# Strassen's seven products for the first layer's branch columns of the input projection

## The chip, the core and the metric

The kernel runs on one core of a Trainium2 chip. A core has five engines that run side by side, each with its own queue of instructions: TensorE (PE in the profile) multiplies matrices into PSUM; VectorE (DVE), ScalarE (ACT) and GpSimd (POOL) do elementwise work; SyncE (SP) issues most of the DMA transfers here. Engines wait for each other through semaphores, and an engine that waits holds up all that stands behind in its queue. The metric is the device time of one execution in microseconds, as the median of several runs.

## The reference

The model is a backbone of two layers over 512 latent tokens and 256 context tokens, all in float32 with 1024 channels. One layer computes:

```
h       = RMSNorm(stream) * (1 + scale) + shift          # shift, scale, gate from SiLU(c) @ w_ada
B C X Z | q k v ZA | GLA q k v r ZG | merge gates = h @ w_in
conv    = B * conv3(C * X) * silu(Z)                     # -> w_br_conv
attn    = attention(q, k, v) * silu(ZA)                  # -> w_br_attn, 8 query heads, 2 key heads
gla     = RMSNorm(gated_linear_attention) * silu(ZG)     # -> w_br_gla, 4 heads, both directions
stream += gate * RMSNorm((sum of sigmoid(merge gate) * branch) @ w_out)
```

In layer 0 latent and context tokens both go on (768 tokens), in layer 1 the output needs the 512 latent ones alone.

## The kernel before, in words

**Products.** A float32 product is carried by three products of shorter parts: each operand is split into a high part, which the multiplier holds exactly, and the rest (`sub_parts`: a cast on ACT, a subtraction on DVE), and `PARTS` lists which parts meet. A column of the input projection (`col_steps`, `gemm_a`, L208) is 128 output channels for all tokens: eight blocks of 128 input channels, three products each, and in layer 0 each product in two pieces of 512 and 256 tokens, so 48 matmuls into one tile `psA` of a ring of three. Its 128 columns of weights are 512 KB, a `Unit`: one DMA into a ring of three `raw` buffers, then a split into a ring of four `hl` buffers.

**Two streams.** The program is a list of `Step`s. The main stream holds the conv columns C, X, Z, B of each of eight channel blocks (`conv_y`), the branch projections (`branch`, with the merge gates' columns), the gated attention (`gated_y`: a ZA column, its SiLU times u, a split) and the last branch (`branch_c`). The side streams hold attention, the four GLA heads (`gla`, with ZG, and levels of decayed blocks: `build` on DVE, one group of products, one masked copy), and the modulation of the next layer (`ada_rows`, L288). `weave` puts side steps between main ones in proportion to the slack that a table gives each. After that every engine has a fixed order. `advance` issues loads and splits of the weights ahead of their steps, as far as the rings allow by a running sum of step costs. Stores go into a list `later` and are issued one step behind.

**Buffers.** Rings in SBUF: H (16 tiles of 128x768), G (16), M (2), `raw` (3), `hl` (4). A tile of a ring can be written again only when all that read its predecessor is done. Attention's and GLA's results `u_att`, `u_gla` and the running sum of the branches `mg` are kept in DRAM and read back.

**The start.** The program loads and normalises the four latent token blocks; the shift and scale of two channel blocks come at a time (`ada_quarter`, L340, four quarters). For each pair of channel blocks the normalised tokens are transposed on PE, scaled and split (`make_h`, `make_h_low`), and the first four columns run piece by piece behind these quarters. The context blocks are normalised meanwhile.

**The end of layer 0.** The last branch's `gating` steps multiply SiLU(ZG) by u_gla, split the product, and the branch's columns `rest` follow. `w_out` then gives the new stream.

## Time and profile before

| | |
|---|---|
| median of 3 runs | 2436.82 us (2435.99 to 2437.19) |
| span of the profiled execution | 2433.6 us |
| PE busy | 2379.5 us, 98%, 14039 matmuls |
| DVE, ACT, POOL busy | 1213.7 (50%), 912.2 (37%), 301.7 us (12%) |
| DMA | 224.26 MB, mean 92 GB/s |
| granted PE clock, mean | 0.995 |

The span runs from the first to the last instruction of one profiled execution; the runs' times also hold what lies around it. Busy shares are means over stages with different limits. In the views that follow, a row of the groups reads: line, engine, operation, output and inputs by the program's names, shapes, count, then busy time and mean duration in ns of one instruction, then the idle time of that engine before them and what ended it. A row of the windows gives for each engine the busy microseconds and the count in one stretch, then the PE clock that was granted, the share of the DMA engines and GB/s. Rows of the chain and of the timeline begin with a start time and a duration. A row on DMA ends with the median time from issue to landing. Layer 0 takes the first 1430 us or so.

### The profile page before, as it was taken

Reading aid. Unit: us, or ns where it says so; the run is one execution under the profiler, and the core shown is the slowest. Engines: PE = TensorE matmul, PEld = TensorE weight load, DVE = VectorE, ACT = ScalarE, POOL = GpSimd, SP = SyncE. Lnnn points to the kernel's source line nnn. Section 1 sums busy time; section 2 is a strip of 40 time slices with the busy share of each in tenths; the row PEclk is TensorE's granted clock in tenths of the full one; section 3 lists DMA queues with packets and bytes.
Section 4 is the critical chain, followed back from the end, with each engine's and each line's share of the span. In section 5 each row is a group of like instructions: output and inputs, shape, how many; then the busy total and the mean of one; then the engine's idle time right before and its main releaser. Section 6 shows DMA issues by size and latency. Waiting matters only on the chain.

```text
span 2433.6 us, 34123 instructions
## 1 busy us (share of the span) xinstructions
PE 2379.5 (98%) x14039; PEld 2059.3 (85%) x14039; DVE 1213.7 (50%) x1910; ACT 912.2 (37%) x1415; POOL 301.7 (12%) x354
## 2 busy tenths in 40 slices
PE   6999999999999999999999989999999999999998
PEld 4899989899988898888988878888888888878877
...
GB/s 244 97 54 52 65 53 77 53 75 76 57 76 119 112 96 128 79 107 84 83 78 99 123 93 97 61 80 88 69 65 87 98 98 122 96 147 62 117 112 109
DMA packets 311080, 224.26 MB, mean 92 GB/s; under 512 B 16600, under 2 KB 281612, under 8 KB 310924
## 3 DMA queue, kind: packets, MB, share of 16 engines
...
q8 instruction: 110, 1.80, 0.3%
...
## 4 chain that ended last, share of the span: by engine, by line
PE 52%; DVE 3%; issue 1%; ACT 1%; DMA 1%; POOL 1%; SPq 0%; POOLq 0%; DVEq 0%; ACTq 0%
PE psA L208 32%; PE psA L216 6%; PE psA L1079 2%; PE psA L716 2%; PE psB L216 2%; PE psB L583 1%; PE psA L824 1%; PE psA L144 1%; PE psA L547 1%; DMA u<-u_gla 1%; DVE hl L125 1%; PE psA L801 1%; PE psB L288 1%; PE psB L1107 1%; ACT junk L158 0%
## 5 line engine op out<-in xcount | busy, mean ns | idle before, releaser
L208 PE MATMUL psA<-hT,hl 128*128 128x512 f32 x5952 | 1211.6, 358 | 3.1 <-DVE hl L125 1.0
L208 PEld LDWEIGHTS psA<-hT,hl 128*128 128x128 f32 x5952 | 967.4, 189 | 177.6 <-issue 15.5
L125 DVE TENSOR_TENSOR hl<-raw,hl 128x1024 fp32r<-128x1024 f32 x258 | 323.2, 1264 | 333.1 <-ACT hl L129 329.9
L129 ACT CAST hl<-raw 128x1024 fp32r<-128x1024 f32 x258 | 266.5, 1047 | 108.8 <-DMA raw<-in_w_in 58.1
L208 PE MATMUL psA<-hi,hl 128*128 128x512 f32 (+1 forms) x1152 | 305.0, 361 | 0.0
L216 PE MATMUL psA<-hl,hT 128*128 128x256 f32 x1920 | 233.7, 283 | 0.0
L216 PEld LDWEIGHTS psA<-hl,hT 128*128 128x128 f32 x1920 | 232.2, 192 | 1.8 <-issue 0.7
L208 PEld LDWEIGHTS psA<-hi,hl 128*128 128x128 f32 x1152 | 190.2, 188 | 35.2 <-issue 1.7
L208 PE MATMUL psA<-lo,hl 128*128 128x512 f32 x576 | 175.1, 358 | 1.1 <-DVE lo L125 1.1
L125 POOL TENSOR_TENSOR rstd<-ms,mhalf 128x1 f32<-128x1 f32 (+4 forms) x54 | 48.8, 904 | 781.2 <-DVE ms L153 632.8
L125 POOL TENSOR_TENSOR Sf<-Sf,a 128x384 f32<-128x384 f32 x56 | 60.8, 1085 | 670.5 <-DVE K L125 425.1
L552 ACT ACTIVATE pe<-psA,nmx 128x768 f32<-128x768 f32 (+1 forms) x80 | 65.4, 817 | 128.1 <-DVE nmx L550 126.0
L208 PEld LDWEIGHTS psA<-lo,hl 128*128 128x128 f32 x576 | 95.0, 188 | 18.1 <-DVE lo L125 1.8
L549 DVE TENSOR_REDUCE mx<-psA 128x1 f32<-128x768 f32 (+1 forms) x80 | 67.8, 847 | 63.5 <-PE psA L547 63.5
L125 DVE TENSOR_TENSOR pTlo<-psA,pThi 128x768 fp32r<-128x768 f32 (+1 forms) x72 | 63.8, 924 | 70.1 <-ACT pThi L129 69.3
L216 PE MATMUL psB<-hl,hT 128*128 128x256 f32 x768 | 94.6, 283 | 0.0
L216 PEld LDWEIGHTS psB<-hl,hT 128*128 128x128 f32 x768 | 93.5, 191 | 1.0
L125 DVE TENSOR_TENSOR sg<-sg,psA 128x768 f32<-128x768 f32 (+1 forms) x48 | 39.3, 819 | 78.9 <-PE psA L208 75.0
L129 ACT CAST pThi<-psA 128x768 fp32r<-128x768 f32 (+1 forms) x72 | 52.8, 779 | 67.7 <-PE psA L144 67.7
L913 POOL TENSOR_SCALAR cv<-u,vec 128x768 f32<-128x768 f32 (+1 forms) x16 | 37.1, 2321 | 307.9 <-DVE u L125 307.9
L464 DVE TENSOR_REDUCE ss<-sq 128x4 f32<-128x512 f32 (+1 forms) x32 | 18.8, 586 | 111.5 <-ACT sq L463 111.5
L125 POOL TENSOR_TENSOR Pb<-Pb,a 128x384 f32<-128x384 f32 x56 | 66.9, 1194 | 0.0
...
## 6 DMA issues: line engine op xcount, KB each, us to landing
raw<-in_w_in SPq DMA_DIRECT2D x192, 512.0 KB, 3.8
raw<-in_w_ada SPq DMA_DIRECT2D x64, 256.0 KB, 2.7
raw<-in_w_br_conv SPq DMA_DIRECT2D x16, 512.0 KB, 4.1
raw<-in_w_br_attn SPq DMA_DIRECT2D x16, 512.0 KB, 4.4
raw<-in_w_br_gla SPq DMA_DIRECT2D x16, 512.0 KB, 4.4
raw<-in_w_out SPq DMA_DIRECT2D x16, 512.0 KB, 4.3
wada<-in_w_ada SPq DMA_DIRECT2D x16, 384.0 KB, 6.5
mg<-sg SPq DMA_DIRECT2D x16, 384.0 KB, 3.7
```

Source lines behind the costliest of these rows:

```text
L125: e.tensor_tensor(out=o, in0=a, in1=b, op=op)
L129: act.copy(out=hi, in_=src)
L144: nc.tensor.transpose(o, i, ident[:n, :n])
L208: mm(ps[:, c0:c0 + wd], lhsT=w[a][:, kb, :], rhs=pair[s], start=(kb == 0 and i == 0), stop=(kb == NK - 1 and i == 2))
L216: mm(ps, lhsT=h_block(kb, tb, a), rhs=w[s][:, kb % 4, :], start=(kb == 0 and i == 0), stop=(kb == NK - 1 and i == 2))
L288: mm(ps[rj:rj + 32, :], lhsT=cst[:, n * i + g, :], rhs=us[n * i + g].raw[j], start=True, stop=True, tile_position=(0, rj))
L547: mm(ps[:, c0:c1], lhsT=Q[j][a][:, qs], rhs=K["k"][b][:, c0:c1], start=(i == 0), stop=(i == 2))
L549: dve.tensor_reduce(out=mx, in_=ps[:, k0:NT], axis=AX.X, op=ALU.max)
L552: act.activation(out=pe[:, k0:], in_=ps[:, k0:NT], func=AF.Exp, bias=nmx, scale=SCALE, accum_out=sm)
L716: mm(ps[:, cs], lhsT=K[:, cs], rhs=Q[:, cs], start=True, stop=True)
L913: pl.tensor_scalar(out=c["cv"][:, :nq], in0=u[:, :nq], scalar1=tap(1), scalar2=None, op0=ALU.mult)
L1079: mm(ps0[tb], lhsT=merged[kb][a][:, ts_], rhs=u0[i].val[b][:, k, :], start=(kb == 0 and z == 0), stop=(kb == NK - 1 and z == 2))
```

## The change

Only layer 0 changes its products. Its columns of the branches (conv C, X, Z, B of channel blocks 1 to 7, the 24 merge gates, ZA and ZG: 68 columns) are made in 34 pairs (`pair_steps`). A pair is two weight blocks of 128 columns, a and b. Input channels are taken in couples of blocks, tokens in two halves of 384. For three of the four couples (`NQ = 3`) the product of a 2x2 arrangement (two columns by two channel blocks, with two token halves) is made by Strassen's scheme in Winograd's form, with seven products instead of eight: p1 to p7, of which p1, p6, p7 and p4 add up in one PSUM bank half U. The fourth couple is multiplied as before (`plain`). All matmuls of a pair are 384 wide, and there are 87 of them where the two columns had 96.

The scheme needs sums of weight blocks, made on POOL in the `raw` buffers (`prep_s`), and sums of token halves of h, made once at the start (`first_h`, tiles TX, 12 of the 16 H tiles). The two operands of the conv product are combined as before. The pairs for Z of the paths and for the merge gates apply their function and store the result in DRAM (`sp0` to `sp5`): y of the conv branch, three gates, two SiLU gates. `load_y` reads y back before branch 0, and u_att and SiLU(ZA) before branch 1; `branch` and `branch_c` read the gates. Now all the pairs come first in the main stream, then the branches.

Besides: h of a channel block is one tile for all 768 tokens; at the start all six token blocks are normalised and transposed before the first modulation quarter; the G ring has 14 tiles, and four of its tiles instead of eight may hold weights ahead of their use; rotary tables are loaded for each pair of query heads; GLA's value columns come after levels 4 and 5; attention and all four heads of layer 0 are woven as one side stream.

```diff
-AHEAD = {"raw": RAW_BUFS, "G": 8, "hl": HL_BUFS, "wo": 4}
+AHEAD = {"raw": RAW_BUFS, "G": 4, "hl": HL_BUFS, "wo": 4, "none": 99}
...
-        return pool.tile([P, NT], dt, tag="G", bufs=16, name=name)
+        return pool.tile([P, NT], dt, tag="G", bufs=14, name=name)
...
+        raws, val = [], {}
+        def start(u, w, c0):
+            u.raw = new_raw()
+            load(out=u.raw.rearrange("p (k c) -> p k c", k=NK), in_=w[:, c0:c0 + P].rearrange("(k p) c -> p k c", p=P))
+            raws.append(u.raw)
+        def blocks(raw, k):
+            return raw[:, :NQ * 256].rearrange("p (q two c) -> p q two c", q=NQ, two=2)[:, :, k, :]
+        def split(n, raw):
+            hl = pool.tile([P, 2, 1024], F32R, tag="hl", bufs=HL_BUFS, name="hl")
+            sub_parts(hl[:, 0, :n], hl[:, 1, :n], raw[:, :n])
+            return lambda kb: [hl[:, s, kb * P:(kb + 1) * P] for s in range(2)]
+        def prep_a(u):
+            val["p"] = split(NQ * 256, raws[0])
+        def prep_s(u):
+            a, b = raws
+            s1 = pool.tile([P, 2, NQ * P], F32R, tag="s1", bufs=2, name="s1")
+            tt(blocks(b, 0), blocks(b, 0), blocks(b, 1), ALU.add, pl)
+            tt(blocks(a, 0), blocks(b, 0), blocks(a, 0), ALU.subtract, pl)
+            tt(blocks(a, 1), blocks(a, 1), blocks(a, 0), ALU.subtract, pl)
+            v = lambda i: s1[:, i, :].rearrange("p (q c) -> p q c", q=NQ)
+            sub_parts(v(0), v(1), blocks(b, 0))
+            tt(blocks(b, 0), blocks(b, 1), blocks(a, 0), ALU.subtract, pl)
+            val["a"] = split(1024, a)
+            val["s1"] = lambda q: [s1[:, s, q * P:(q + 1) * P] for s in range(2)]
+        def prep_d(u):
+            val["d"] = split(1024, raws[1])
+        ua = Unit(lambda u: start(u, wa, ca), prep_a)
+        us = Unit(lambda u: start(u, wb, cb), prep_s)
+        ud = Unit(lambda u: None, prep_d, ring="none", ns=0.0)
+        ua.until, us.until = us, ud
...
+        qs, rest = range(NQ), range(2 * NQ, NK)
+        half = lambda kb, t: [hTa[kb][:, s, t * HN:(t + 1) * HN] for s in range(2)]
+        x = lambda i: [TX[i][q] for q in qs]
+        def run(ps, ws, xs, start=True, stop=True):
+            n = len(ws)
+            for j in range(n):
+                for z, (a, b) in enumerate(PARTS):
+                    mm(ps, lhsT=ws[j][a], rhs=xs[j][b], start=(start and j == 0 and z == 0), stop=(stop and j == n - 1 and z == 2),
+                       skip_group_check=True)
+        def plain(ps, name, t, start=False):
+            if len(rest):
+                run(ps, [val[name](kb) for kb in rest], [half(kb, t) for kb in rest], start=start)
...
+            st["U"], st["V"] = A[:, :HN], A[:, 512:512 + HN]
+            st["ab"], st["cd"] = M(name="ab"), M(name="cd")
+            st["c"] = H(name="c")
+            run(st["U"], [val["p"](2 * q) for q in qs], [half(2 * q, 0) for q in qs])
+            act.copy(out=st["ab"][:, :HN], in_=st["U"])
+        def p2():
+            run(st["V"], [val["p"](2 * q + 1) for q in qs], [half(2 * q + 1, 0) for q in qs])
+        def p6():
+            run(st["U"], [val["a"](2 * q) for q in qs], x(2), start=False)
+            act.copy(out=st["ab"][:, HN:], in_=st["U"])
+        def r11():
+            plain(st["V"], "a", 0)
+            tt(st["c"][:, :HN], st["V"], st["ab"][:, :HN], ALU.add)
+        def p7():
+            run(st["U"], [val["d"](2 * q) for q in qs], x(3), start=False)
+            act.copy(out=st["cd"][:, :HN], in_=st["U"])
+        def p5():
+            run(st["V"], [val["s1"](q) for q in qs], x(1))
+            act.copy(out=st["cd"][:, HN:], in_=st["V"])
+            tt(st["ab"][:, HN:], st["ab"][:, HN:], st["cd"][:, HN:], ALU.add, pl)
+        def p3():
+            W = psB()[:, :HN]
+            run(W, [val["a"](2 * q + 1) for q in qs], [half(2 * q + 1, 1) for q in qs])
+            plain(W, "a", 1)
+            tt(st["c"][:, HN:], W, st["ab"][:, HN:], ALU.add)
+        def r22():
+            plain(st["V"], "d", 1)
+            tt(st["cd"][:, HN:], st["V"], st["cd"][:, :HN], ALU.add)
+        def p4():
+            run(st["U"], [val["d"](2 * q + 1) for q in qs], x(4), start=False)
+            plain(st["U"], "d", 0)
+            evac(st["c"], st["cd"][:, HN:], st["U"])
...
+        def get(kb):
+            tiles = [M(name="u")] + [pool.tile([P, NT], F32, tag="s1", bufs=2, name="z") for _ in srcs[1:]]
+            for x, src in zip(tiles, srcs):
+                load(out=x, in_=src[kb * P:(kb + 1) * P, :])
+            if len(srcs) > 1:
+                tt(tiles[0], tiles[0], tiles[1], ALU.mult)
+            return tiles[0]
+        split = lambda kb: Y.append(split_to(t.pop(kb), NT))
+        S = []
+        for kb in range(NK + 1):
+            if kb < NK:
+                S.append(Step(lambda kb=kb: t.__setitem__(kb, get(kb)), cost=spread))
+            if kb > 0:
+                S.append(Step(lambda kb=kb - 1: split(kb), cost=spread))
+        return S
...
+            def before(st, c=c, rows=rows, tile_of=tile_of):
+                if sg_d is not None:
+                    c["sg"] = M(name="sg")
+                    load(out=c["sg"], in_=sg_d[rows, :])
...
-            Y[kb] = split_to(sz[kb][:, :nq], nq, G)
+            v = new_h().rearrange("p (s n) -> p s n", s=2)
+            Y[kb] = v[:, 0, :], v[:, 1, :]
+            sub_parts(v[:, 0, :nq], v[:, 1, :nq], sz[kb][:, :nq])
...
+    def raw_h(kb):
+        h_base[kb] = new_h()
+        h_views(kb, 0)
+        f = x0T[kb] = (M if kb < 2 else G)(name="x0T")
+        ps = psA()
+        for tb in range(6):
+            tr(ps[:, tb * P:(tb + 1) * P], xn[tb][kb // 4][:, (kb % 4) * P:(kb % 4 + 1) * P])
+        if kb % 2:
+            act.copy(out=f, in_=ps[:, :NT])
+        else:
+            dve.tensor_copy(out=f, in_=ps[:, :NT])
+    def first_h(q, vec):
...
+        f, T_ = x0T, {}
+        def scaled():
+            for kb in (2 * q, 2 * q + 1):
+                for t, c in ((0, slice(0, NLAT)), (1, slice(NLAT, NT))):
+                    sc, sh = vec["sc"][:, t, kb:kb + 1], vec["sh"][:, t, kb:kb + 1]
+                    dve.tensor_scalar(out=f[kb][:, c], in0=f[kb][:, c], scalar1=sc, scalar2=sh, op0=ALU.mult, op1=ALU.add)
+                act.copy(out=hTa[kb][:, 0, :], in_=f[kb])
+        def sums():
+            if q >= NQ:
+                return
+            g, h = f[2 * q], f[2 * q + 1]
+            for i in (1, 3):
+                t = pool.tile([P, 2, HN], F32, tag="s1", bufs=2, name="t")
+                T_[i], T_[i + 1] = t[:, 0, :], t[:, 1, :]
+            x = lambda i: T_[i]
+            lo, up = slice(0, HN), slice(HN, NT)
+            tt(x(1), g[:, up], g[:, lo], ALU.subtract)
+            tt(x(3), h[:, up], g[:, up], ALU.subtract)
+            tt(x(2), h[:, up], x(1), ALU.subtract)
+            tt(x(4), h[:, lo], x(2), ALU.subtract)
+        def low():
+            for kb in (2 * q, 2 * q + 1):
+                tt(hTa[kb][:, 1, :], f[kb], hTa[kb][:, 0, :].bitcast(F32), ALU.subtract)
+        def parts():
+            for i in (2, 1, 3, 4):
+                if q < NQ:
+                    v = H(F32R, name="tx").rearrange("p (s n) -> p s n", s=2)
+                    sub_parts(v[:, 0, :], v[:, 1, :], T_[i])
+                    TX[i][q] = [v[:, 0, :], v[:, 1, :]]
+        return [Step(scaled), Step(sums), Step(low), Step(parts)]
...
-    prog += norm_steps(tbs[:4])
-    prog += quarters[0][0] + ctx_norm[:2] + [quarters[0][1]] + h0[0][:2] + ctx_norm[2:] + h0[0][2:] + sv[:1]
+    prog += norm_steps(tbs) + [Step(lambda kb=kb: raw_h(kb)) for kb in range(NK)] + sv[:1]
...
+            prog += q0 + [f0] + h0[0][:1] + [split(C)] + h0[0][1:]
...
+        if l == 0:
+            pairs, gates, paths = first_projections(vec, y_d[0], y_d[1:4], y_d[4:])
+            early, gating, rest = branch_c(l, nq, u_gla, vec, mg_dram, merged, sz, y_d[3], y_d[5])
+            main = weave(gates[0] + paths[0] + gates[1] + paths[1] + gates[2] + load_y([y_d[0]], Ya, 500.0) +
+                         branch(l, nq, 0, "w_br_conv", Ya, vec, mg_dram, y_d[1]), mods_next)
+            last = branch(l, nq, 1, "w_br_attn", Yb, vec, mg_dram, y_d[2])
+            for kb in range(6):
+                last.insert(len(last) - 11 + 2 * kb, gating[kb][0])
+            main = conv + pairs + main + load_y([u_att, y_d[4]], Yb, 500.0) + last
+            for s in main:
+                s.cost = max(s.cost, 1.0)
+            side = att + sum(heads, [])
+            side.insert(len(side) - 12, early[0])
+            side.insert(len(side) - 12, early[1])
+            prog += weave(main, side)
+            prog += [gating[kb][1] for kb in range(8)] + [rest[0], rest[4], rest[1], rest[5], rest[2], rest[6], rest[3], rest[7]] + rest[8:]
```

PE at the start, before: the transposes (L144, `x`) of the first channel blocks follow the first quarter (L340).

```order
L144 MATMUL psB<-ident,crow 128x40
L340 MATMUL psB<-wada,cst 32x256 x16
L144 MATMUL psB<-ident,mod 128x64 x2
L144 MATMUL psB<-ident,x_97 128x128
L144 MATMUL psB<-ident,x_101 128x128
L144 MATMUL psB<-ident,x_105 128x128
```

PE at the start, now: the last five of 48 transposes (L148), the quarter (L470) and the first column (L226).

```order
L148 MATMUL psA<-ident,x_108 128x128
L148 MATMUL psA<-ident,x_112 128x128
L148 MATMUL psA<-ident,x_116 128x128
L148 MATMUL psA<-ident,x_132 128x128
L148 MATMUL psA<-ident,x_136 128x128
L470 MATMUL psB<-wada,cst 32x256 x16
L148 MATMUL psB<-ident,mod 128x64 x2
L226 MATMUL psA<-hT,hl 128x512
```

The quarter stood ahead of all transposes, and now stands behind all of them.

PE at a modulation step of layer 1 in the middle of layer 0, before (L288): the column on both sides uses the same split weights, `hl_6770`.

```order
L208 MATMUL psA_6981<-hT_280,hl_6770 128x512
L208 MATMUL psA_6981<-hT_303,hl_6770 128x256
L288 MATMUL psB_6996<-raw_6624,cst_69 32x512 x2
L288 MATMUL psB_6996<-raw_6767,cst_69 32x512 x2
L208 MATMUL psA_6981<-hT_393,hl_6770 128x512
L208 MATMUL psA_6981<-hT_400,hl_6770 128x256
```

PE at such a step now (L418), inside a pair: p2, a GLA level (L845), the step, and p6 with `hl_8442`, a split of the pair's second form of a.

```order
L311 MATMUL psA_8384<-hT_249,hl_8381 128x384 x3
L311 MATMUL psA_8384<-hT_269,hl_8381 128x384 x3
L845 MATMUL psA_8409<-Q_8264,K_8267 128x128 x6
L418 MATMUL psB_8427<-raw_8210,cst_69 32x512 x2
L418 MATMUL psB_8427<-raw_8242,cst_69 32x512 x2
L311 MATMUL psA_8384<-tx_365,hl_8442 128x384 x3
L311 MATMUL psA_8384<-tx_462,hl_8442 128x384 x3
```

And SP's queue there now: `raw_8210` and `raw_8242` are the step's weights, the sp5 rows stores of the pair before, and `raw_8433` is the second weight block of the pair whose p6 is shown.

```order
L403 DMA raw_8210<-in_w_ada 128x512 x2
L403 DMA raw_8242<-in_w_ada 128x512 x2
L1077 DMA sp5_81<-c_8196 128x768
L1077 DMA sp5_81<-e2_8375 128x768
L262 DMA raw_8433<-in_w_in 128x8x128
```

The step now stands inside a pair, and the block that p6 needs is the next to use a buffer of the `raw` ring after the step's two.

DVE between two blocks of the gated attention, before: product with u (`sz`), its split (`lo`), and then nine instructions of GLA, vectors and weights up to the next product.

```order
L125 TENSOR_TENSOR sz_6787<-sz_6787,u_6555 128x768
L125 TENSOR_TENSOR lo_6791<-sz_6787,hi_6790 128x768
L125 TENSOR_TENSOR a_6444<-a_6444 128x384
L125 TENSOR_TENSOR a_6451<-a_6451 128x384
L125 TENSOR_TENSOR Q_6818<-q_6438,a_6444 128x192x2
L125 TENSOR_TENSOR Q_6818<-q_6438,a_6451 128x192x2
```

DVE at the same work now, the `load_y` before branch 1 (blocks 1 to 5 of eight).

```order
L129 TENSOR_TENSOR hl_10848<-raw_10619,hl_10848 128x1024
L129 TENSOR_TENSOR lo_10854<-u_10816,hi_10853 128x768
L129 TENSOR_TENSOR u_10857<-u_10857,z_10858 128x768
L129 TENSOR_TENSOR lo_10863<-u_10825,hi_10862 128x768
L129 TENSOR_TENSOR u_10866<-u_10866,z_10867 128x768
L129 TENSOR_TENSOR lo_10872<-u_10857,hi_10871 128x768
L129 TENSOR_TENSOR u_10875<-u_10875,z_10876 128x768
L129 TENSOR_TENSOR lo_10881<-u_10866,hi_10880 128x768
L129 TENSOR_TENSOR u_10884<-u_10884,z_10885 128x768
L129 TENSOR_TENSOR lo_10890<-u_10875,hi_10889 128x768
```

The eight blocks now follow each other, and the product of a block stands between the product and the split of the block before it.

170 lines of the change are left out of this document (132 added, 38 removed).

## The prediction

> **What bounds the kernel now.** I read the page first, for who is busy and who ends last.
>
> ```profile
> span 2433.6 us, 34123 instructions
> ...
> PE 2379.5 (98%) x14039; PEld 2059.3 (85%) x14039; DVE 1213.7 (50%) x1910; ACT 912.2 (37%) x1415; POOL 301.7 (12%) x354
> ...
> PE 52%; DVE 3%; issue 1%; ACT 1%; DMA 1%; POOL 1%; SPq 0%; POOLq 0%; DVEq 0%; ACTq 0%
> ```
>
> PE is busy 98% of the span and the chain that ends last is mostly PE. DVE, ACT and POOL have half or more of their time free. Then the windows, cut at the start, the body of layer 0, the change of layers and layer 1:
>
> ```profile
> core 0: us, PE busy (x) PEld busy (x) DVE busy (x) ACT busy (x) POOL busy (x), PEclk, DMA share, GB/s
> 0.00:25.00 25.00, 9.14 (x48) 4.42 (x48) 10.25 (x37) 12.78 (x30) 4.40 (x13) 0.93 0.94 314
> 25.00:80.00 55.00, 49.92 (x303) 36.27 (x304) 20.13 (x44) 17.67 (x31) 12.85 (x17) 0.94 0.44 141
> 80.00:1280.00 1200.00, 1194.43 (x7597) 1063.64 (x7597) 570.35 (x886) 417.64 (x638) 133.17 (x144) 1.00 0.27 81
> ```
>
> From 80 to 1280 us PE lacks only 5.6 us of being busy all the time, at full clock. So two things follow. Products taken out of that stretch are gained nearly one to one, and every new wait of PE costs its full length, since no idle time is there to absorb it. The forecast is one sum: the products saved, less the waits that the new order opens.
>
> **Products saved (A).** The chain's longest pieces price a product.
>
> ```profile
> 1016.42 11.52 PE psA L216 x96
> ...
> 1283.29 66.70 PE psA L208 x376
> 1349.98 16.49 PE psA L1079 x72
> ```
>
> The L208 piece alternates 512 and 256 wide, 384 on average: 66.70 / 376 = 0.177 us. L216 (256 wide) is 11.52 / 96 = 0.120 and L1079 (512 wide) 16.49 / 72 = 0.229. A pair now takes 87 products of 384 where two columns took 96 of mean width 384, so it saves nine: 9 x 0.177 x 34 pairs = 54 us. A straight 384 has no row; halfway between 0.120 and 0.229 it is 0.1745, and then a pair costs 15.2 against 17.0 us, 63 us in all. I take 57, nearer to the measured mixed piece, with ends 54 and 63.
>
> The Trainium skill (TensorE: Matmul & The Clock Gate, "Wait — 56ns, not 53.3ns?") prices a warm product at its columns divided by 2.4 GHz plus about 2.5 ns. By it the nine products are not all gain, because a mixed couple becomes cheaper than the trace has it, and A would be an estimated 50 us. The rows 0.229 and 0.120 are above its 0.216 and 0.109, so the rows stand.
>
> **What a pair adds beside PE.** These are the rows (by form).
>
> ```profile
> L125 DVE TENSOR_TENSOR hl<-raw,hl 128x1024 fp32r<-128x1024 f32 x258 | 323.2, 1264 | 333.1 <-ACT hl L129 329.9
> L125 DVE TENSOR_TENSOR lo<-sz,hi 128x768 fp32r<-128x768 f32 x24 | 22.5, 958 | 14.5 <-ACT hi L129 14.5
> L125 DVE TENSOR_TENSOR sz<-sz,u 128x768 f32<-128x768 f32 x14 | 15.0, 1069 | 25.9 <-ACT sz L956 13.2 <-DMA u<-u_gla 12.6
> L125 DVE TENSOR_TENSOR Q<-q,a 128x384 f32<-128x384 f32 x56 | 28.6, 552 | 0.0
> L129 ACT CAST hl<-raw 128x1024 fp32r<-128x1024 f32 x258 | 266.5, 1047 | 108.8 <-DMA raw<-in_w_in 58.1 <-PE psA L208 36.6 <-DMA raw<-in_w_br_attn 9.5
> L129 ACT CAST hi<-sz 128x768 fp32r<-128x768 f32 x24 | 19.5, 834 | 42.5 <-DVE sz L125 42.5
> L125 POOL TENSOR_TENSOR Sf<-Sf,a 128x384 f32<-128x384 f32 x56 | 60.8, 1085 | 670.5 <-DVE K L125 425.1 <-ACT a L679 245.4
> ```
>
> DVE gets two more splits (0.958 + 0.552) and three 384-wide adds where two column evacuations stood (3 x 0.552): about 3.2 us. ACT gets as much in casts and copies, POOL five adds of about 1.09, 5.4 us. In 34 pairs that is 108 us on DVE and 184 on POOL: 570 + 108 of about 1150 us is 59%, POOL 28%. None becomes a bound on average, so this work costs nothing where PE has products queued; without that cover each 3.2 us per pair would be 109 us. What can show is order within a pair. p6 and p7 add into the same bank U, and the copy of U after p6 is covered by r11 alone: six products, 1.05 us. A copy of some 0.5 us (an estimate, a little over half of the 0.834 cast) fits unless a 1.047 cast stands before it on ACT, and then p7 waits about 0.6. At one such wait in three pairs that is 7 us (**F**); never is 0, and I keep 2 to 15.
>
> **The start (B).** PE's timeline:
>
> ```profile
> 12.06 5.49 PE L340 MATMUL psB<-wada,cst 128*32 128x256 f32 x32 [7.64 <-DMA wada<-in_w_ada]
> ...
> 20.90 0.63 PE L144 MATMUL psB<-ident,x 128*128 128x128 f32 x4 [1.91 <-DVE sc L309]
> 22.93 0.45 PE L144 MATMUL psB<-ident,x 128*128 128x128 f32 x1 [1.40 <-DVE x L1197]
> 23.63 0.90 PE L144 MATMUL psB<-ident,x 128*128 128x128 f32 x3 [0.26 <-DVE x L1197]
> 24.19 0.78 PE L208 MATMUL psA<-hT,hl 128*128 128x512 f32 x1
> ...
> 67.86 15.07 PE L208 MATMUL psA<-hT,hl 128*128 128x512 f32 x84
> ```
>
> Before, the first modulation quarter runs from 12.06 in PE's idle time while the context blocks are still being normalised (their transposes wait for DVE until 22.9 and 23.6). Now all 48 transposes stand ahead of it. The last context block is ready at about 23.6, its last transposes end at about 25, the quarter takes 5.5 (to 30.5), the scale column comes 3.3 later (before: 17.55 to 20.90), and then come two scalings, the cast (0.8 each) and semaphores: first product near 36 instead of 24.19, 12 us later. Per quarter DVE gets four 384-wide sums (2.2 us) ahead of the low parts, while PE is spared twelve transposes (four take 0.63, so 1.9 us); these about cancel. The first four columns then end near 88 instead of 67.86 + 48 x 0.179 = 76.4. B = 12, ends 7 (the transposes of the latent blocks fill the wait) and 18 (the sums show in all three quarters).
>
> **Four pairs behind modulation steps (C).** DMA rows, issue to landing:
>
> ```profile
> raw<-in_w_in SPq DMA_DIRECT2D x192, 512.0 KB, 3.8
> ...
> mg<-sg SPq DMA_DIRECT2D x16, 384.0 KB, 3.7
> ...
> u<-u_att SPq DMA_DIRECT2D x8, 384.0 KB, 4.2
> ...
> x<-o SPq DMA_DIRECT2D x4, 256.0 KB, 2.0
> ```
>
> The modulation rows of layer 1 (L418) hold two of the three raw buffers until PE has used them. At four of them the pair's second weight block is loaded into just such a buffer. From the end of that step until p6 can run: load 3.8, three POOL adds 3.3, cast 1.05, subtract 1.26, together 9.4 us. In the PE order p6 stands directly behind the step in one case and 1.6 to 3.8 us of products behind it in three. Waits: 9.4 + 7.8 + 5.6 + 5.6 = 28; less a little for shorter landings, C = 27, ends 12 (half hidden) and 34.
>
> **The reload for branch 0 (D).** Eight blocks come back through two M buffers: per two blocks 4.2 + 0.83 + 0.96 = 6.0 us, so 24, and about 4 more where SP has the last stores in front: the last block is ready some 28 us after the last pair. PE has a burst of 96 products of 256 (11.5 us) and 1.6 of others ahead of the column, and the column itself is 48 x 0.177 = 8.5 us, 1.1 per block. Undisturbed it would end at 21.6; waiting for the last block, at 29. D = 8, ends 2 and 13.
>
> **The reload for branch 1 (E).** Here each block needs two loads and a multiplication, and in DVE's order the multiplication of block k+1 stands ahead of the subtraction of block k. That subtraction frees the M buffer for block k+2, so only one block is under way at a time: 4.2 (load) + 1.07 (sz by u) + 0.96 (subtract) = 6.2 us. Count from the end of branch 0's last product. The second M buffer holds that column's gate tile: evacuation 0.9, store 3.7, load 4.2, multiply 1.1, subtract 1.0 bring block 0 to 11 us. Block 1 waits for the third load and for eight operations of a GLA level and a weight split on DVE (5.6 us): 23. Blocks 2 to 6 follow at 6.2 each: 54; block 7 one us later; its products end at 56. PE has in that time the column itself (8.5) and two level steps (0.7 each): 9.9. The wait is E = 46. Before, u was loaded a column ahead, each multiplication followed by its own subtraction, and the sz row names a wait for u only at u_gla, 12.6 us in all. Ends: 28 if two loads land in 2.0 us, as fast as the quickest row above (eight times 2.2 less), and 57 if they disturb each other and take 5.5.
>
> Behind gaps of this kind the clock falls:
>
> ```profile
> 20.00:25.00 5.00, 2.40 (x9) 1.43 (x9) 4.82 (x15) 2.60 (x5) 0.54 (x1) 0.67 1.11 359
> 25.00:30.00 5.00, 4.06 (x11) 2.86 (x11) 2.40 (x3) 3.04 (x6) 3.14 (x5) 0.50 1.11 369
> 30.00:40.00 10.00, 8.97 (x58) 5.28 (x58) 3.72 (x11) 1.80 (x4) 2.48 (x5) 0.90 1.10 377
> ```
>
> After the waits of the start PE got 0.50 for 5 us and 0.90 for the next 10: 2.5 + 1.0 = 3.5 us lost behind one gap. Inside E it costs nothing, since 1.1 us of products at half speed still fit the 6.2 of a block. The Trainium skill (same page, "HAM oscillation — how this bites in real kernels") states that idle gaps of PE over some 3.4 us put it back to half clock, each time anew. It speaks against this change, whose E has seven such gaps; the trace of the start agrees with the 0.50.
>
> **The rest (G).** At the end of layer 0 the gated channels of branch 2 now go through the h tiles, all ahead of the first product: 8 x 0.96 = 7.7 us of DVE, against 7.8 us of wait that the chain shows there before:
>
> ```profile
> 1271.41 7.80 issue
> ```
>
> Layer 1's products stay; its G ring is two smaller and POOL has more rope tables, 64-wide, of 0.4 us. G = 0, ends -5 and +5.
>
> **Sum**: -57 + 12 + 27 + 8 + 46 + 7 + 0 = +43. From the profiled span, 2433.6 + 43 = 2477; the median 2436.8 lies 3.2 above that span, so 2480.
>
> **The rivals.**
> 1. The reads are covered (faster). C, D and E rest on what I take to be queued in front of PE. If the side streams stand there and the loads land early, so that those three together stay at 10 us, the time is 2436.8 - 57 + 12 + 10 + 7 = 2409. It decides from C + D + E below 38 (forecast: 81). For: DMA was used 27% in the body, and 2.0 us landings exist. Against: the serial chain in E alone keeps 28 at that landing. Chance 0.25.
> 2. C, D and E at 33 to 43: no difference, 2437. Chance 0.07.
> 3. The pair's own order binds. If both copies of U (after p6 and p7) met a cast in every pair, 0.6 x 2 x 34 = 41 instead of 7: 2514. For: ACT casts are the largest group of ACT. Against: ACT has 60% free, and p7's copy has the 30 products of p5, p3 and r22 as cover, 5.3 us. Chance 0.07.
> 4. The clock after gaps: five gaps (four of C, one of E) at 3.5 us are 17 more: 2497. For: the rows above. Against: the start's gap was longer (7.64 before the quarter, then a broken stream) than three of C's four. Chance 0.13. This is the mechanism behind the rule of the Trainium skill cited under E.
>
> **Chances and range.** My forecast has 0.48, rivals 3 and 4 0.20: slower 0.68, same 0.07, faster 0.25 (0.2%, 5 us, is about what can be told from no change). The forecast's own range is 2455 to 2500. The whole reaches 2407 below, just past rival 1, and 2510 above, short of rival 3; the ends of all terms at once (-17 and +88 to the span) would be wider still.
>
> **What would show it.** Right: L311 products at 0.175 to 0.178 us (A); the first product after 35 us (B); waits of PE at L311 for hl after L418, four of 5 to 10 us (C); one stretch of some 55 us where PE is busy a fifth, with DVE waiting for u and z and SP for DVE (E). Wrong: if PE's busy digits stay 9 through layer 0, C and E fall and the time is near 2409; a wait of over 0.5 us in front of p7 in most pairs is rival 3; a clock below 0.9 behind each gap is rival 4; L311 above 0.185 takes 25 us or more from A.

## The result, and the profile after

| | before | after |
|---|---|---|
| median of 4 runs | 2437.01 us (2435.99 to 2437.87) | 2834.31 us (2830.11 to 2838.49) |
| span of the profiled execution | 2433.6 us | 2836.5 us |
| ratio of the times | | 1.1635, 95% interval 1.1619 to 1.1651 |

The kernel became 16% slower. The direction was forecast and the size was not: 2480 us were expected, 2510 was the end of the range. The page of the changed kernel:

```profile
span 2836.5 us, 34624 instructions
...
PE 2471.7 (87%) x13733; PEld 2166.1 (76%) x13733; DVE 1348.7 (48%) x2130; ACT 1031.5 (36%) x1655; POOL 498.9 (18%) x552
...
PE   5878789897977687787994979999999999999998
...
PEclk9998999998989898889996989999999999999999
```

There are 306 matmuls fewer, the nine of each of 34 pairs, and still PE is busy 92 us longer. Its idle time rose from 2433.6 - 2379.5 = 54 to 2836.5 - 2471.7 = 365 us. The 403 us that the span grew are therefore 311 of new idle time and 92 of products that ran longer, although there are fewer of them. The digits of PE show where: not in one stretch, but in nearly every slice of the first half. The windows give the sizes (columns as in the prediction), first of before, then of after:

```profile
120.00:1160.00 1040.00, 1034.43 (x6551) 917.54 (x6550) 492.38 (x770) 375.90 (x576) 101.89 (x100) 1.00 0.27 80
1283.00:1430.00 147.00, 143.93 (x739) 120.99 (x739) 74.80 (x110) 53.34 (x102) 16.93 (x26) 1.00 0.36 115
1430.00:2433.00 1003.00, 979.44 (x5341) 832.19 (x5341) 535.83 (x832) 408.21 (x613) 133.30 (x154) 0.99 0.32 93
```

```profile
120.00:1160.00 1040.00, 841.89 (x4817) 778.78 (x4816) 461.15 (x739) 390.43 (x658) 247.98 (x243) 0.90 0.22 66
1160.00:1364.00 204.00, 165.41 (x902) 149.02 (x902) 79.69 (x126) 75.36 (x116) 44.63 (x45) 0.91 0.24 76
1480.00:1560.00 80.00, 43.52 (x206) 35.75 (x205) 39.62 (x55) 9.71 (x11) 11.35 (x10) 0.70 0.42 142
1560.00:1832.00 272.00, 245.06 (x1309) 209.40 (x1308) 127.10 (x186) 72.36 (x134) 26.32 (x38) 0.94 0.43 140
1832.00:2836.00 1004.00, 978.21 (x5331) 831.97 (x5330) 532.05 (x827) 405.57 (x610) 142.82 (x171) 0.99 0.32 94
```

The pairs run from 117 to 1364 us. Between 120 and 1364 PE is idle for 198 + 39 = 237 us, where the same kind of work before left 5.6 us idle in 1040, and the granted clock falls from 1.00 to 0.90. The reload before branch 1 (1480 to 1560) has 36 us of idle time, the branches behind it 27, and layer 1 is as it was. Between 120 and 1160 us DVE, ACT and POOL are busy 461, 390 and 248 of 1040 us (44%, 38%, 24%): no engine has become the bound. What PE waited for in the pairs' stretch (117 to 1364 us; total, times, longest):

```profile
PE psA L311 <- DVE cd L129: 72.0, 27, 8.8
PE psA L311 <- DVE c L129: 49.9, 29, 5.8
PE psA L311 <- ACT ab L324: 40.9, 19, 6.2
PE psA L311 <- ACT hl L133: 33.8, 6, 8.3
PE psA L311 <- ACT ab L331: 12.8, 21, 1.5
PE psA L311 <- ACT cd L339: 11.0, 14, 2.5
```

Five of these six rows are waits for work that reads PSUM: the copies after p1 (L324), p6 (L331) and p7 (L339), and the additions that take V after r11 (`c`) and after r22 (`cd`). Together 187 us. The prediction has none of them; it has 7 us for p7 behind the copy after p6. One pair's end and the next one's beginning show what they are. PE's timeline (start, duration, what, then the idle time ahead and what ended it):

```profile
639.42 1.21 PE L311 MATMUL psA<-hT,hl 128*128 128x384 f32 x6
646.44 3.25 PE L311 MATMUL psA<-tx,hl 128*128 128x384 f32 x9 [5.81 <-DVE cd L129]
649.48 3.84 PE L311 MATMUL psA<-hT,hl 128*128 128x384 f32 x15
659.51 3.25 PE L311 MATMUL psA<-hT,hl 128*128 128x384 f32 x9 [6.19 <-ACT ab L324]
662.56 3.06 PE L311 MATMUL psA<-tx,hl 128*128 128x384 f32 x9
666.18 1.31 PE L311 MATMUL psA<-hT,hl 128*128 128x384 f32 x6 [0.57 <-ACT ab L331]
668.22 1.86 PE L311 MATMUL psA<-tx,hl 128*128 128x384 f32 x9 [0.72 <-DVE c L129]
```

The rows are, in order: r22 (six products into V), p4 (nine into U), then p4's last six with the next pair's p1 (nine), p2, p6, r11, p7. p4 writes U, and it waits 5.81 us for the addition that reads V. p2 writes V, and it waits 6.19 us for the copy that reads U. r11 writes V and waits for the copy of U after p6; p7 writes U and waits for the addition that reads V. U and V are two separate banks, but they are two halves of one tile `psA`, and the program orders a write of the tile behind every read of the tile that came before it. The arithmetic asks for none of these waits. And each lasts until the reader is done, with all that stands ahead of it in its queue. The same stretch on POOL, ACT and DVE (a few rows of each left out):

```profile
641.25 3.21 POOL L129 TENSOR_TENSOR raw<-raw 128x384 f32<-128x384 f32 x3 [1.43 <-issue]
```

```profile
643.54 1.04 ACT L133 CAST hl<-raw 128x1024 fp32r<-128x1024 f32 x1 [3.17 <-POOL raw L129]
...
653.56 1.28 ACT L166 ACT_TABLE_LOAD   x1
...
656.40 1.14 ACT L572 ACTIVATE xh<-psA,rstd 128x128 f32<-128x128 f32 x4
...
658.90 0.56 ACT L324 COPY ab<-psA 128x384 f32<-128x384 f32 x1
```

```profile
644.61 1.22 DVE L129 TENSOR_TENSOR hl<-raw,hl 128x1024 fp32r<-128x1024 f32 x1 [3.03 <-ACT hl L133]
...
645.83 0.55 DVE L129 TENSOR_TENSOR cd<-psA,cd 128x384 f32<-128x384 f32 x1
```

V was complete at 640.6. The addition that reads it takes 0.55 us, but on DVE it stands behind the subtraction of a weight split, which waits for the cast on ACT, which waits for sums on POOL (the cast starts as the second of the row's three ends). So p4 stands until 646.4. At 658.90 it is ACT that is late, with a table load, a cast and the activations of attention's rotary ahead of the copy. Engines that are half idle on average were late where it counted.

The clock shows in the same stretch (windows of 6 us and less):

```profile
659.50:665.50 6.00, 5.99 (x18) 5.62 (x18) 3.88 (x8) 0.69 (x1) 1.83 (x2) 0.50 0.54 190
665.50:670.00 4.50, 3.21 (x17) 2.74 (x17) 2.16 (x3) 1.84 (x3) 1.47 (x2) 1.00 0.00 0
```

Behind the wait of 6.19 us PE ran at half clock for 6 us, nine products in 3.25 us; behind the wait of 0.72 us nine take 1.86.

The reload before branch 1, PE:

```profile
1494.99 1.50 PE L845 MATMUL psA<-Q,K 128*128 128x128 f32 x12
...
1517.19 1.01 PE L226 MATMUL psA<-lo,hl 128*128 128x512 f32 x2 [9.21 <-DVE lo L129]
...
1531.55 1.01 PE L226 MATMUL psA<-lo,hl 128*128 128x512 f32 x2 [4.21 <-DVE lo L129]
...
1537.60 1.01 PE L226 MATMUL psA<-lo,hl 128*128 128x512 f32 x2 [3.76 <-DVE lo L129]
1544.01 1.01 PE L226 MATMUL psA<-lo,hl 128*128 128x512 f32 x2 [4.12 <-DVE lo L129]
...
1552.73 0.49 PE L226 MATMUL psA<-hi,hl 128*128 128x512 f32 x1
```

From the third block on, one comes every 6.0 to 6.4 us, and the column's products end at 1553.2, 58 us after branch 0's last product. And the start:

```profile
38.00 1.01 PE L226 MATMUL psA<-hT,hl 128*128 128x512 f32 x2 [4.27 <-ACT hl L133]
...
84.52 10.51 PE L226 MATMUL psA<-hT,hl 128*128 128x512 f32 x58 [0.38 <-DVE hT L129]
```

The first product starts at 38.0, and the first four columns end at 95.0.

### The profile page after: what moved, and what is told of

It is laid out like the page before. It is cut to its first block, busy times and chain, and to the rows that moved or that the text cites. A ratio compares the mean times of both kernels' runs of the same rounds, so it can differ in the third digit from the quotient of the medians.

```text
span 2836.5 us, 34624 instructions
## 1 busy us (share of the span) xinstructions
PE 2471.7 (87%) x13733; PEld 2166.1 (76%) x13733; DVE 1348.7 (48%) x2130; ACT 1031.5 (36%) x1655; POOL 498.9 (18%) x552
## 5 line engine op out<-in xcount | busy, mean ns | idle before, releaser
L226 PE MATMUL psA<-hT,hl 128*128 128x512 f32 x3264 | 726.5, 377 | 17.0 <-DVE hT L129 9.7
L226 PEld LDWEIGHTS psA<-hT,hl 128*128 128x128 f32 x3264 | 566.8, 190 | 130.4 <-DVE hT L129 12.1
L129 DVE TENSOR_TENSOR hl<-raw,hl 128x1024 fp32r<-128x1024 f32 (+1 forms) x292 | 358.4, 1237 | 370.7 <-ACT hl L133 367.1
L311 PE MATMUL psA<-tx,hl 128*128 128x384 f32 x918 | 229.1, 403 | 153.5 <-DVE cd L129 72.0
L133 ACT CAST hl<-raw 128x1024 fp32r<-128x1024 f32 (+1 forms) x292 | 294.7, 1022 | 135.8 <-PE psA L226 51.6
L311 PEld LDWEIGHTS psA<-tx,hl 128*128 128x128 f32 x918 | 192.5, 229 | 178.4 <-DVE cd L129 81.3
L311 PE MATMUL psA<-hT,hl 128*128 128x384 f32 x1224 | 270.0, 365 | 61.1 <-ACT ab L324 40.9
L311 PEld LDWEIGHTS psA<-hT,hl 128*128 128x128 f32 x1224 | 229.6, 205 | 82.6 <-ACT ab L324 48.4
L226 PE MATMUL psA<-hi,hl 128*128 128x512 f32 (+1 forms) x768 | 216.5, 377 | 12.7 <-ACT hi L133 7.8
L129 POOL TENSOR_TENSOR raw<-raw 128x384 f32<-128x384 f32 x136 | 149.9, 1106 | 271.0 <-issue 137.4
L226 PEld LDWEIGHTS psA<-hi,hl 128*128 128x128 f32 x768 | 133.4, 198 | 41.0 <-ACT hi L133 8.8
L226 PE MATMUL psA<-lo,hl 128*128 128x512 f32 (+1 forms) x384 | 122.0, 373 | 32.6 <-DVE lo L129 32.6
L226 PEld LDWEIGHTS psA<-lo,hl 128*128 128x128 f32 x384 | 66.0, 196 | 47.5 <-DVE lo L129 37.1
L311 PE MATMUL psB<-hT,hl 128*128 128x384 f32 x510 | 96.4, 340 | 0.0
L311 PEld LDWEIGHTS psB<-hT,hl 128*128 128x128 f32 x510 | 90.1, 190 | 1.0 <-issue 0.8
```

The costliest lines, as they stand in the source:

```text
L129: e.tensor_tensor(out=o, in0=a, in1=b, op=op)
L133: act.copy(out=hi, in_=src)
L226: mm(ps[:, c0:c0 + wd], lhsT=w[a][:, kb, :], rhs=pair[s], start=(kb == 0 and i == 0), stop=(kb == NK - 1 and i == 2))
L311: mm(ps, lhsT=ws[j][a], rhs=xs[j][b], start=(start and j == 0 and z == 0), stop=(stop and j == n - 1 and z == 2), skip_group_check=True)
```

## The experiments

The theory after the result: most of the loss is the order inside a pair, that is, waits between U and V that come from the one tile. The rivals: the loss is the reload (E) and the modulation steps (C), larger than thought; or the engines beside PE are late whatever the tile says, because their queues are full of weight sums and table loads. Each run below is one execution beside one of the kernel before on the same chip (2435.00 to 2438.97). Single executions of the changed kernel lie within 8.4 us of each other, so differences under some 8 us are not read as effects.

**The waits between U and V taken away.** Every product of p2, r11, p7, p5, r22 and p4 is declared independent of the readers of the other bank; what it has to wait for in its own bank is named explicitly. Instructions and their order stay. Two of the six places:

```diff
         def p2():
-            run(st["V"], [val["p"](2 * q + 1) for q in qs], [half(2 * q + 1, 0) for q in qs])
+            ms = run(st["V"], [val["p"](2 * q + 1) for q in qs], [half(2 * q + 1, 0) for q in qs])
+            apart(ms, [st["c1"]], [])
...
         def p7():
-            run(st["U"], [val["d"](2 * q) for q in qs], x(3), start=False)
-            act.copy(out=st["cd"][:, :HN], in_=st["U"])
+            ms = run(st["U"], [val["d"](2 * q) for q in qs], x(3), start=False)
+            apart(ms, [st["v11"]], [st["c6"]])
+            st["c7"] = act.copy(out=st["cd"][:, :HN], in_=st["U"])
```

> The changed kernel, same instructions in the same order on every engine; only the waits between the two accumulators U and V of a pair are taken away. They lie in two banks of one PSUM tile, and the order has each product into the one wait for the copy or the addition that reads the other; the waits on the same accumulator stay. Theory T (the shared tile): the idle time ahead of p2, r11, p7, p5 and p4, 212 us in the changed kernel, falls below 50, the products at half clock become few, and the time falls by 200 to 300 us, to 2530 to 2630. Rival R (the copies are late for their own reader, because ACT and DVE are queued up): the idle time only moves to p6, p7 and p4, which wait for the copy of U anyway; the time stays above 2750. Rival H (the clock itself, not waits): the waits fall but a sixth of the products stays at half clock; about 2650 to 2750.

Measured: 2678.65 us, 156 less than the changed kernel's median: 49 above the end of theory T, far from rival R, and inside the range of rival H. H's sign is not there, though: the products that start 320 ns apart, as at half clock, fell from 362 to 200 of 2652. Of the 160 us by which the span fell, 102 are idle time of PE and 57 are products that ran faster. PE's waits:

```profile
PE psA L311 <- ACT hl L133: 37.6, 8, 8.3
PE psA L311 <- ACT ab L332: 35.2, 10, 9.3
PE psA L226 <- DVE lo L129: 30.8, 9, 9.2
PE psA L311 <- DVE c L129: 27.4, 15, 7.7
```

What remains at L311 are waits that the arithmetic needs: p6 for the split weights `hl`, p6 for the copy of U after p1 (its line is 332 here), p5 for the addition that reads V after r11. Added up over the pairs (from the start of the product before to that of the piece, less 174 ns, so a little above the sums of the waits), the time lost in front of p2, r11, p7 and p4 fell from 45, 18, 55 and 77 us to 0.7, 1.6, 3.4 and 0.9; in front of p6 it rose from 31 to 70, in front of p5 from 16 to 27. So the mechanism of T is shown, and it is the largest single cause that any run took away: the order by tile alone costs 156 us. It is not most of the loss of 397 us. Some 50 us of the false waits came back as true waits for the same late queues. The Trainium skill (PSUM — Partial Sum Buffer, "PSUM bank collisions raise a hardware error") states that two engines collide only when they touch the same bank; by it these waits guard nothing. In this run PE writes one bank while another engine reads the other, and it is 156 us shorter.

**The reload with each product directly ahead of its own split.** The loads go ahead, the multiplication moves into the split's step:

```diff
-            if len(srcs) > 1:
-                tt(tiles[0], tiles[0], tiles[1], ALU.mult)
-            return tiles[0]
-        split = lambda kb: Y.append(split_to(t.pop(kb), NT))
+            t[kb] = tiles
+        def split(kb):
+            tiles = t.pop(kb)
+            if len(srcs) > 1:
+                tt(tiles[0], tiles[0], tiles[1], ALU.mult)
+            Y.append(split_to(tiles[0], NT))
```

> The changed kernel, with the reload before branch 1 reordered alone: the two loads of a block are issued ahead, and its product stands directly before its own split, no longer ahead of the split of the block before. Term E as predicted: the stretch from the end of branch 0 to the eighth block, 58 us in the changed kernel, becomes 11 plus seven times about 3.6, some 36 us; the time falls by 15 to 28 us. Rival (landing bounds: 768 KB per block keep the period at 6 us): under 5 us.

Measured: 2822.26, 12 less, below the 15 to 28 that were expected. The pairs end at 1362.8 us, 1 us earlier than before, and the part behind them takes 1457 us instead of 1473. The stretch itself fell from 58 to 40 us (36 were expected). So the serial chain of E (a multiplication ahead of the split that frees its buffer) is real; a better order takes back 15 us of it.

**Layer 1's modulation out of the pairs,** woven into branch 0 alone:

```diff
-            main = weave(gates[0] + paths[0] + gates[1] + paths[1] + gates[2] + load_y([y_d[0]], Ya, 500.0) +
-                         branch(l, nq, 0, "w_br_conv", Ya, vec, mg_dram, y_d[1]), mods_next)
+            main = gates[0] + paths[0] + gates[1] + paths[1] + gates[2] + load_y([y_d[0]], Ya, 500.0)
+            main += weave(branch(l, nq, 0, "w_br_conv", Ya, vec, mg_dram, y_d[1]), mods_next)
```

> The changed kernel, with the modulation steps of layer 1 moved out of the pairs into branch 0's columns, nothing else. Term C as predicted: the idle time ahead of p6, 31 us in the changed kernel, falls under 10 and the time by 15 to 30 us. Rival (p6 waits for its weights for other reasons, or the other waits take the time up): the idle time ahead of p6 stays above 20, or falls while the time changes by under 8 us.

Measured: 2852.64, 18 more: a miss. The waits of p6 went (31 to 6 us) and the pairs ended 34 us earlier, at 1329.8, but what follows took 1521 us instead of 1473. The first reload is now bare:

```profile
1342.28 1.01 PE L226 MATMUL psA<-hi,hl 128*128 128x512 f32 x2 [5.38 <-ACT hi L133]
```

In the changed kernel the largest wait there is 2.25 us, here it is this one of 5.38. Most of the 34 us were not waits. PE's idle time within the pairs fell only from 237 to 231 us, because in front of p7 and p5 the waits rose from 61 to 91; some 18 us are products that now stand behind the pairs (12 of them the modulation's), and the rest are products at a better clock. Behind the pairs the idle time rose from 68 to 89. So the waits of C are there in their size, but they stood in front of false waits that take their place when they go, and the steps were cover for the reload D.

**All three together.**

> All three edits together: no waits between U and V, product by split in the reload, modulation late. If the three causes are separate, their gains add up: with theory T, 2490 to 2590. What is left above the kernel before (2437) is then the start (+19 us in the changed kernel's trace) and what none of the three touches.

Measured: 2666.04, 12.6 below the first of them alone, and 76 above the upper end of what was expected: a miss. Without false waits the next thing in line decides, and that is the queues of DVE and ACT: p5 waits 43 us for the addition after r11, p6 31 us for the copy of U. The longest wait of the pairs is one of these, 9.33 us, and on ACT (first fence) that copy has two table loads, a cast and the rotary's activations ahead of it.

```profile
576.83 1.28 ACT L1135 ACT_TABLE_LOAD   x1 [1.88 <-DVE cd L129]
...
580.04 1.28 ACT L166 ACT_TABLE_LOAD   x1
...
585.39 0.56 ACT L332 COPY ab<-psA 128x384 f32<-128x384 f32 x1
```

```profile
586.00 3.25 PE L311 MATMUL psA<-tx,hl 128*128 128x384 f32 x9 [9.33 <-ACT ab L332]
```

The next four runs start from the version without false waits (2678.65) and ask which queue it is.

**No table loads in the pairs:** SiLU and the sigmoid replaced by the exponential, whose table is loaded anyway. Two of the places:

```diff
-                act.activation(out=z, in_=z, func=AF.Silu)
-                exp_table()
+                act.activation(out=z, in_=z, func=AF.Exp)
...
-        gates = [act_pairs(O_MG + b * D, sg_d[b], AF.Sigmoid, V_GATE + 8 * b) for b in range(3)]
+        gates = [act_pairs(O_MG + b * D, sg_d[b], AF.Exp, V_GATE + 8 * b) for b in range(3)]
```

> The kernel without waits between U and V, and in its pairs SiLU and Sigmoid replaced by Exp, the function that attention and GLA use, so that ACT loads no function table for a pair and none back (two loads of 1.28 us and a one-element Exp in most pairs; the values are no longer the reference's). Theory Q1 (what is left ahead of p6 and p5, 70 and 27 us, are copies of U that stand on ACT behind the evacuation of the pair before, with its two table loads): the idle time ahead of p6 falls below 35 and the time by 40 to 80 us, from 2679 to 2600 to 2640. Rival Q2 (they stand behind casts that wait for the weight sums of POOL): under 15 us.

Measured: 2648.01, 31 less, between the two forecasts; the time in front of p6 stayed above 50. ACT's busy time fell by 74 us (1029.9 to 955.6), so under half of it had been in PE's way. Most of these loads are no work that the change added: the traces have 102 table loads before, 113 in the changed kernel and 59 in this run. So this run also takes away what the kernel before paid and covered.

**No weight sums on POOL:**

```diff
-            tt(blocks(b, 0), blocks(b, 0), blocks(b, 1), ALU.add, pl)
-            tt(blocks(a, 0), blocks(b, 0), blocks(a, 0), ALU.subtract, pl)
-            tt(blocks(a, 1), blocks(a, 1), blocks(a, 0), ALU.subtract, pl)
             v = lambda i: s1[:, i, :].rearrange("p (q c) -> p q c", q=NQ)
             sub_parts(v(0), v(1), blocks(b, 0))
-            tt(blocks(b, 0), blocks(b, 1), blocks(a, 0), ALU.subtract, pl)
```

> The kernel without waits between U and V, and the four sums of weight blocks on POOL left out of each pair (so the products are taken with the blocks as loaded, and the result is not the reference's): the casts and subtractions of a pair's weights no longer wait for POOL. Theory Q2 (ACT and DVE stand at casts that wait for POOL, with copies and additions queued behind them): the idle time ahead of p6 and p5, 97 us together, falls below 50 and the time by 40 to 90 us. Rival Q1 (tables): under 15 us.

Measured: 2605.15, 74 less, as theory Q2 has it, though the time in front of p6 and p5 fell from 97 to 61 and not below 50. POOL was busy 497.6 of 2677 us, 19%, and 146 us of that, the four sums of 34 pairs, cost 74 us of time.

**The copies after p1 and p6 on DVE instead of ACT:**

```diff
-            st["c1"] = act.copy(out=st["ab"][:, :HN], in_=st["U"])
+            st["c1"] = dve.tensor_copy(out=st["ab"][:, :HN], in_=st["U"])
...
-            st["c6"] = act.copy(out=st["ab"][:, HN:], in_=st["U"])
+            st["c6"] = dve.tensor_copy(out=st["ab"][:, HN:], in_=st["U"])
```

> The kernel without waits between U and V, with the copies of U after p1 and p6 on DVE instead of ACT; nothing left out. Theory Q1: the copy after p1 no longer stands behind table loads, and the idle time ahead of p6 falls by 20 to 40 us, the time by as much. Rival Q2: DVE stands at subtractions that wait for the same casts, so the waits only change engine, and the time stays within 15 us.

Measured: 2712.49, 34 more: a miss for both.

```profile
PE psA L311 <- DVE ab L332: 66.4, 13, 13.0
```

The wait for this copy was 35.2 us behind ACT's queue and is 66.4 behind DVE's. DVE holds the subtractions of the weight splits, which wait for the casts and these for POOL's sums.

**Neither table loads nor weight sums.**

> Both left out: no table loads and no weight sums in the pairs. If both queues count separately, the gains of the two single runs add up (2679 less 80 to 150 us); if one covers the other, the sum is clearly less. What then remains above 2437 is not within a pair's copies: the start, the reloads, and the clock.

Measured: 2566.12, 113 less, and 31 + 74 = 105: these two add.

The next four ask for the start and the reload (again from 2678.65).

**The ZA columns back as single columns,** each with its product with u and its split, as before; 30 pairs are left.

```diff
-            main = weave(gates[0] + paths[0] + gates[1] + paths[1] + gates[2] + load_y([y_d[0]], Ya, 500.0) +
+            main = weave(gates[0] + gates[1] + paths[1] + gates[2] + load_y([y_d[0]], Ya, 500.0) +
...
-            main = conv + pairs + main + load_y([u_att, y_d[4]], Yb, 500.0) + last
+            main = conv + pairs + main + gated_y(l, nq, O_ZA, u_att, Yb) + last
```

> The kernel without waits between U and V (2679 us), with the eight ZA columns taken out of the pairs and made again one by one as before the change, each column with its u, product and split (30 pairs are left). Theory of term E (the reload stalls because the columns that covered it, 8.5 us each, were moved into the pairs): the 58 us stretch between branch 0 and branch 1 goes, about 48 us; four pairs fewer give up 4 x 1.9 = 7.5 us of products and save their own waits (178 / 34 = 5 us each, 20 us): 2600 to 2640. Rival (the loads or the M ring bound it wherever it stands): the gain is under 20 us.

Measured: 2633.72, 45 less, as expected. The waits for `lo` (30.8 us) leave the list of large ones: eight columns had been the cover of the reload, and the change had moved them into the pairs. But the 45 are not E alone. Between the pairs and layer 1 PE's idle time fell from 65 to 46 us, since steps of GLA now wait there, and within the pairs, of which four are gone, from 138 to 118.

**The first modulation quarter ahead of the context blocks and the transposes,** as it stood before.

```diff
-    prog += norm_steps(tbs) + [Step(lambda kb=kb: raw_h(kb)) for kb in range(NK)] + sv[:1]
+    prog += norm_steps(tbs[:4]) + quarters[0][0] + norm_steps(tbs[4:]) + [Step(lambda kb=kb: raw_h(kb)) for kb in range(NK)] + sv[:1]
...
-            prog += q0 + [f0] + h0[0][:1] + [split(C)] + h0[0][1:]
+            prog += [f0] + h0[0][:1] + [split(C)] + h0[0][1:]
```

> The kernel without waits between U and V, with the products of the first modulation quarter moved ahead of the context blocks' norm and of all 48 transposes, as they stood before the change. Term B (the quarter was moved behind them): the first column comes 5 to 9 us earlier, the time falls by 5 to 12 us. Rival (DVE's scalings and sums, or the loads of the context blocks, bound the start): under 3 us.

Measured: 2682.27, no gain. The first product came earlier, at 32.45 instead of 36.32 in the run it starts from,

```profile
32.45 1.01 PE L226 MATMUL psA<-hT,hl 128*128 128x512 f32 x2 [4.27 <-ACT hl L133]
```

the pairs began at 112.0 instead of 114.9, and they ended at 1204.6 against 1204.3. Three microseconds earlier at the start were gone by the end. They lie within the spread of single runs, but they fit pairs that do not run at PE's pace: what PE gains ahead of them it waits for inside.

**Both together.**

> Both of these together: the gains add up, 2590 to 2635. It is the fastest complete version tried here; the kernel before at 2436 stays faster by 150 us or more.

Measured: 2628.85, the fastest version that leaves nothing out. The kernel before stays 190 us ahead of it.

**The weights' splits placed later in the queues** (the planner's load time 3500 to 7000 ns), so that they stand less in front of copies and additions.

```diff
-LOAD_NS = 3500.0
+LOAD_NS = 7000.0
```

> The kernel without waits between U and V, with 7.0 instead of 3.5 us of the plan's time given to a load before its split is queued, so that fewer casts stand on ACT and DVE waiting for POOL's sums. If early queueing is what blocks the copies: p6 and p5 wait less than their 97 us, and the time falls by 20 to 50 us. Rival (with three raw buffers the second block of a pair comes so late that its split is forced when it is needed): no change within 15 us, or slower.

Measured: 2688.54, 10 more. The time lost in front of p5 fell from 27 to 13 us, that in front of p6 rose from 70 to 73, and the pairs ended at 1205.6. Moving the splits only shifts which product is late.

Two runs price what is left.

**The false waits with empty queues:** the changed kernel with its waits between U and V, without table loads and sums. Compared with the run without tables, sums and false waits (2566.12) it prices the waits without queues.

> The changed kernel, with its waits between U and V kept, but without table loads and weight sums in the pairs (the values are not the reference's). It tells what the shared tile costs by itself. If it is bare latency (five waits a pair of a 0.48 us copy or 0.56 us addition and its semaphores, some 0.75 us each): 34 x 5 x 0.75 = 128 us above the 2566 of the same kernel without these waits, 2680 to 2710. If its 156 us came from queues (the copy it waits for stands behind tables and casts): within 70 us, below 2640.

Measured: 2736.08, 170 above, which is 5.0 us in each of 34 pairs. That is above both forecasts.

```profile
PE psA L307 <- DVE cd L129: 50.8, 27, 4.7
PE psA L307 <- DVE c L129: 44.5, 29, 4.3
PE psA L307 <- ACT ab L320: 20.8, 19, 4.8
```

The queues lengthen these waits (72.0, 49.9 and 40.9 in the changed kernel), but the waits do not come from them. With the false order, PE stands still at up to five places of a pair until a reader has ended; the products run slower as well (PE is busy 63 us longer than without the false waits).

**All of it at once:** no false waits, tables or sums, and the ZA columns single.

> No waits between U and V, no table loads, no weight sums, and the ZA columns one by one again (values not the reference's). If the four causes are separate, the 45 us of the ZA columns come off the 2566: 2510 to 2530. What is then left above 2436 has to lie in the start (30 us more of lost PE time than before), in the tail of layer 0 (some 50) and in the pairs' other waits, less the 56 us of products that 30 pairs save.

Measured: 2536.77, above what was expected: 29 less, where the ZA columns alone had given 45. This is still 100 us above the kernel before:

```profile
PE 2376.3 (94%) x13769; PEld 2101.5 (83%) x13769; DVE 1314.7 (52%) x2110; ACT 944.2 (37%) x1548; POOL 344.7 (14%) x412
```

Its span is 2535.0, so PE is idle 159 us against 54, and the products saved are eaten by slower ones. That rest is spread (the start, remaining waits in the pairs, the branches behind them), and no run takes it apart further. With the table loads, most of which the kernel before had too, it would be larger (without the sums alone 2605.15 were measured, without both 2566.12: 39 us). A tile of V's own, which would be the plain mend of the false waits, was not run: a pair would hold two of the three `psA` tiles, and attention and GLA share them.

## Why the prediction was wrong

**Term F failed.** The prediction wrote that the copy of U after p6 "is covered by r11 alone" and that p7 then waits about 0.6 us in one pair of three. That took for granted that r11, which writes V, can run while U is copied, and the same for p2 under the copy after p1, p5 under the copy after p7, and p4 under the addition of r22. It can't: the tile orders them, and so the very piece that was counted as cover is the one that waits. 7 us were priced, 41 in rival 3; the waits of five pieces measure 187 us, and taking them away gives 156 in the full kernel and 170 with empty queues. Rival 3 named the place but not the mechanism. Its sign came (p7 waits over 0.5 us in 29 of 34 pairs), but p7 waits there for the addition that reads V, not for a copy that a cast delays. The order of the instructions gave no hint of it: the pieces stand as the text describes. The dependency is in what each instruction waits for, and the one place that shows it ahead of a run is the line that takes U and V from the same tile.

**"None becomes a bound on average, so this work costs nothing where PE has products queued" failed too.** With the false waits gone, the sums on POOL cost 74 us, the table loads on ACT 31, both together 113. The table loads have no term in the prediction at all: it counts casts, copies and additions. Most of them are older than the change, and what is new is that PE stands behind them. The condition in that sentence was the weak point: PE has no products queued in a pair, since each piece needs a split, a copy or an addition that came shortly before it, and these stand in line behind unrelated work. The text worked out 109 us as the price of DVE's additions without cover, and then set it aside for a 59% average. That 109 lies near 113 is chance: these are other engines' work, and what counted was their place in a queue, not their sum.

**A was right.** Single matmuls 384 wide start 174 ns apart where nothing disturbs them, the middle that was worked out from the two other widths (174.5). 34 x (17.03 - 87 x 0.174) = 64 us saved, one above the upper end; 57 was used. The time doesn't show it, because in the pairs it is not PE's pace that decides.

**B was too small and mattered less.** The first product came at 38.0 (36), the four columns ended at 95.0 (88): 19 us late where 12 were priced, just beyond the end of 18. In the run with the quarter first, a start 3 us earlier changes nothing at the end of the pairs, so it seems that B is not a term of a sum any more.

**C had its mechanism and its size:** behind four modulation steps p6 waits 4.5 to 8.3 us for its split, 25 us against 27. But it is not additive either: with the modulation moved, the pairs' idle time fell by 6 us alone, and the time rose. **D** is 4 us instead of 8 (2.25 in its largest wait), because the modulation covers it.

**E was right in its chain, its period and its end:** 6.0 to 6.4 us a block against 6.2, the products' end 58 us after branch 0's against 56, which is 48 us more than PE's own 10 us of work there. That 45 us came back with the cover, near the 46 of the sum, is in part luck, since four pairs went with it; with all else left out it was 29.

Read off the trace one by one, A to E come to -64 + 19 + 25 + 4 + 48 = 32 us, against 36 in the sum. So the miss lies in the other 370 of the 403 us, for which the sum had the 7 of F.

**G** holds for layer 1: 978 busy of 1004 us against 979 of 1003. But the branches behind the reload (1560 to 1832) have 27 us idle that no term has; before, 147 us of such work had 3. They were not tested by themselves.

**Rival 4, the clock, is larger than it was priced** (17 us), because gaps came in most pairs and not in five places. Of 2652 products that directly follow another of their piece, 362 start 320 ns behind it, 174 + 146: 53 us in the pairs. Another 159 start 245 to 295 ns behind; nearly all of them are the second product of a piece, so these 16 us are not put down to the clock. The Trainium skill (TensorE: Matmul & The Clock Gate, "HAM oscillation — how this bites in real kernels") says that gaps over some 3.4 us bring half clock each time; the traces agree for long gaps, with 0.50 behind the gap of 6.19 us and full pace behind that of 0.72. In the changed kernel's trace the products fell to 320 ns apart behind all 20 waits of over 3.5 us in front of a piece, but behind 11 of the 21 waits of 2 to 3 us they did so too.

How the 403 us of span come together can be told only in part, since the terms overlap: the false waits with the clock that falls behind them are 156 to 170, queues of sums and tables up to 113 (not all of it new work), the ZA columns' lost cover 29 to 45 at most, and the rest, 100 us after all of these are taken out, already holds the products saved. What this rest consists of stays open.
